# Copies out of PSUM issued on ScalarE ahead of the last pair's remaining activations, and a second buffer for sums of weights, in the seven-product FFN of a hybrid decoder block

## The chip, the cores and the metric

The kernel runs on one core of a Trainium2 chip, as one program without loops at run time. Its engines are TensorE (PE, with weight loads listed as PEld), VectorE (DVE), ScalarE (ACT), GpSimd (POOL) and SyncE (SP, which here issues DMAs only). The metric is the device time of one execution in microseconds; less is better. Engines run their own instructions strictly in the order written, and wait for each other by semaphores.

## The reference

A decoder block for 1024 tokens of width 1024: two token mixers, their merge, and then the part that matters here, a gated FFN with a causal convolution of width 3 along the tokens (`D_FF` = 2816, that is 22 tiles of 128 features for the gate half and 22 for the value half):

```
def conv_ffn(h, w_up, conv_w, conv_b, w_down):
    u = h @ w_up
    T = u.shape[1]
    up = jnp.pad(u, ((0, 0), (CONV_WIDTH - 1, 0), (0, 0)))
    u = sum(up[:, i:i + T] * conv_w[i] for i in range(CONV_WIDTH)) + conv_b
    gate, val = jnp.split(u, 2, axis=-1)
    return (jax.nn.gelu(gate, approximate=True) * val) @ w_down
```

All is float32. A float32 product is made of three products of rounded parts: each operand is split into a high part (`hi`) and the remainder (`lo`), and `mm3` issues high times high, high times low and low times high for each 128 deep slice.

## The kernel before

Features lie on the partitions and tokens along the free dimension, in two halves of 512 tokens. Tile `j` of the gate half and tile `j` of the value half of `w_up` form a pair. Three pairs (`NSTD`) are computed the plain way by `up_std`. The other 19 pairs run in the loop that the change is in. There the product of a 2 by 2 block of weights (two halves of the depth, gate and value) with a 2 by 2 block of activations (two halves of the depth, two token halves) is made with seven block products in place of eight, out of sums of weights and sums of activations. A block product is four slices of depth, three matmuls each, so 12 matmuls, and a pair has 84. The first four of the 19 pairs (`NEAR`) have two of their seven products made earlier and stored in DRAM (`e_d`); they have 60 matmuls and load the two results.

PE's order in a pair is: `pX` first half (weights `w1`), `pZ` (weights `w2`), `pT` (`w2`), `pY` (`w3`), then `pX` second half, `pZ` again (`w3`) and `pT` again (`w4`). The second use of a bank adds to what the first left there, so the first result must have been read before: `s1` is a copy of `pX` by ACT (L1183), `s5` a copy of `pZ` by ACT (L1188), and `s5 = pT + s5` is a DVE addition (L1190). After it come `s1 = pY + s1` (L1192, DVE), the copy of the second `pX` into `ub` (L1195, ACT), the POOL addition of `s1` and `s5` (L1196) and the DVE additions of `pZ` and `pT` to `s1` (L1198, L1200). These give the four tiles of `u`: two feature tiles, two token halves, in `ub`.

Then each of the four tiles goes through `conv`: one ACT activation (L1063) and two DVE operations (L1064, L1066). `gate` takes the two convolved tiles of a token half: gelu on ACT (L1071), their product on DVE (L1072) and a DMA to `f_d`, issued from ACT's own queue (L1073).

The weights of a pair come in by two DMAs on SP's queue (`st1`, L1148, and `st2`, L1150, two buffers each). DVE makes the sums in four operations (`sa` in L1163 and L1164, then in place L1166 and L1167), ACT makes the high parts and POOL or DVE the low parts (`cut`, L1159 and L1160): POOL for `w1`, for `w2` (out of `sa`) and for both halves of `w3`, DVE for `w4`. `sa` has one buffer, so L1163 of the next pair waits until ACT and POOL have read the one before. The low parts of `w1` and `w2` share three buffers, those of `w3` and `w4` two; the high parts of `w1` and `w3` share three, those of `w2` and `w4` two.

The two buffers of `st2` are free again when DVE has made the low part of `w4`; only then does SP issue the load for the next pair but one.

The order on each engine comes from a scheduler that plays the program through its own timing and takes, among what is ready, what has the highest priority. Priority is the place in the program's text, except that the weights' block stands in `tc.high_priority(offset=WPRIO)`, 500 instructions ahead. What runs on the chip is the order so fixed.

Of the kernel before, what the change touches and what calls it, by code (L numbers as in the profile page):

```python
# [9 lines left out]
F32 = mybir.dt.float32  # L10
# [148 lines left out]
def body(tc, nc, xT, xN, pos, wch, wbrw, wbret, wout, wup, wdn, w2a2, gw2, rows, vecs, consts0, consts1, out):  # L159
    V, S, G, PE = nc.vector, nc.scalar, nc.gpsimd, nc.tensor  # L160
    ctx = ExitStack()

    @contextmanager
    def tile_pool(**kw):
        with tc.tile_pool(**kw) as pool:
            yield Lines(pool)

    with ctx:
# [18 lines left out]
        def VC(name):  # L187
            o, n = VOFF[name]
            return vct[:, o:o + n]
# [5 lines left out]
        def bank(name, tag="A"):  # L195
            return psB.tile([128, 512], F32, tag=tag, name=name, bufs=BANKS[tag])
# [69 lines left out]
        wx = pz.tile([128, 2, KT, 128], F32R, tag="BKp", name="w_x")  # L266
# [60 lines left out]
        with pctx, tile_pool(name="p1", bufs=1, reuse_waits="tile", side="right") as p1:  # L327
# [159 lines left out]
            n = gp.tile([128, 512], F32, tag="rt", name="nrot", bufs=1)  # L487
# [551 lines left out]


        bp = ctx.enter_context(tile_pool(name="bp", bufs=1, reuse_waits="tile"))
        ectx = ExitStack()
        b12 = ectx.enter_context(tile_pool(name="b12", bufs=1, reuse_waits="tile"))
        es = ectx.enter_context(tile_pool(name="es", bufs=2, reuse_waits="tile"))

        w3s = ectx.enter_context(tile_pool(name="w3s", bufs=1, reuse_waits="tile"))
        wpools[:] = [(wp, (2, 3, 2)), (w3s, (1, 1, 1)), (wp, (2, 3, 2))]
        f_d = dp.tile([2, FT, 128, 512], F32, name="f_d")
        carry = cp.tile([128, 2 * NSTD, 2], F32, name="carry", bufs=1)
# [5 lines left out]
        def mmb(ps, w, ks, B, first, last):  # L1055
            mm3(ps, [(w[0][:, k, :], w[1][:, k, :], B[n][0], B[n][1]) for n, k in enumerate(ks)],
                first=first, last=last, skip=not first)

        def conv(pool, ub, b, j, src):

            i = j + FT * b
            u = pool.tile([128, 512], F32, tag=f"u{b}", name="u_f")
            S.activation(u, src, AF.Identity, bias=VC("cb")[:, i:i + 1], scale=VC("cw2")[:, i:i + 1])  # L1063
            V.scalar_tensor_tensor(out=u, in0=ub[:, 1:513], scalar=VC("cw1")[:, i:i + 1], in1=u,  # L1064
                                   op0=ALU.mult, op1=ALU.add)
            V.scalar_tensor_tensor(out=u, in0=ub[:, 0:512], scalar=VC("cw0")[:, i:i + 1], in1=u,  # L1066
                                   op0=ALU.mult, op1=ALU.add)
            return u

        def gate(j, hf, u0, u1):  # L1070
            S.activation(u0, u0, AF.Gelu_apprx_tanh)  # L1071
            V.tensor_tensor(out=u0, in0=u0, in1=u1, op=ALU.mult)  # L1072
            nc.scalar.dma_start(f_d[hf, j], u0)  # L1073
# [63 lines left out]
        wx = ctx.enter_context(tile_pool(name="wx", bufs=1, reuse_waits="tile", side="right"))  # L1137
# [3 lines left out]
        fp = fctx.enter_context(tile_pool(name="fp", bufs=2, reuse_waits="tile"))  # L1141
        W8 = [128, 8, 128]
        lh, rh_ = slice(0, 4), slice(4, 8)

        for n, j in enumerate(range(NSTD, FT)):
            with tc.high_priority(offset=WPRIO):
                st1 = wp.tile(W8, F32, tag="ws", name="w_st", bufs=2)
                nc.sync.dma_start(st1, wup[j])  # L1148
                st2 = wx.tile(W8, F32, tag="ws", name="w_st", bufs=2)
                nc.sync.dma_start(st2, wup[j + FT])  # L1150
                sa = wx.tile(W8, F32, tag="sa", name="w_sa")
                if n >= NEAR:
                    w1 = wp.tile(W8, F32R, tag="wh", name="w_hi", bufs=3), wx.tile(W8, F32R, tag="wl", name="w_lo", bufs=3)
                w2 = wx.tile(W8, F32R, tag="wh", name="w_hi", bufs=2), wx.tile(W8, F32R, tag="wl", name="w_lo", bufs=3)
                w3 = wp.tile(W8, F32R, tag="wh", name="w_hi", bufs=3), wp.tile(W8, F32R, tag="wl", name="w_lo", bufs=2)
                w4 = wx.tile(W8, F32R, tag="wh", name="w_hi", bufs=2), wp.tile(W8, F32R, tag="wl", name="w_lo", bufs=2)

                def cut(w, ks, src, eng):
                    S.copy(w[0][:, ks, :], src)  # L1159
                    eng.tensor_tensor(out=w[1][:, ks, :], in0=src, in1=w[0][:, ks, :], op=ALU.subtract)  # L1160
                if n >= NEAR:
                    cut(w1, slice(0, 8), st1, G)
                V.tensor_tensor(out=sa[:, lh, :], in0=st2[:, lh, :], in1=st2[:, rh_, :], op=ALU.add)  # L1163
                V.tensor_tensor(out=sa[:, rh_, :], in0=st1[:, lh, :], in1=st2[:, lh, :], op=ALU.subtract)  # L1164
                cut(w2, slice(0, 8), sa, G)
                V.tensor_tensor(out=st2[:, lh, :], in0=sa[:, lh, :], in1=st1[:, lh, :], op=ALU.subtract)  # L1166
                V.tensor_tensor(out=st1[:, rh_, :], in0=st1[:, rh_, :], in1=st2[:, lh, :], op=ALU.subtract)  # L1167
                cut(w3, lh, st2[:, lh, :], G)
                cut(w3, rh_, st1[:, rh_, :], G)
                cut(w4, lh, st2[:, rh_, :], V)  # L1170
            if n >= NEAR:
                pX = psA.tile([128, 512], F32, tag="a", name="ps_x")
            pZ = bank("ps_z", "B")
            pT = bank("ps_t", "CY"[n % 2])
            pY = bank("ps_y", "AI"[n % 2])
            ub = [fp.tile([128, 1026], F32, tag=f"ub{b}", name="ub") for b in range(2)]
            for b in range(2):
                G.memset(ub[b][:, 0:2], 0.0)
            s1 = fp.tile([128, 512], F32, name="s1")
            s5 = fp.tile([128, 512], F32, name="s5")  # L1180
            if n >= NEAR:
                mmb(pX, w1, range(4), hn2[0][0:4], True, True)
                S.copy(s1, pX)  # L1183
            else:
                nc.sync.dma_start(s1, e_d[n, 0])
                nc.sync.dma_start(ub[0][:, 2:514], e_d[n, 1])
            mmb(pZ, w2, range(4), T1, True, True)
            S.copy(s5, pZ)  # L1188
            mmb(pT, w2, range(4, 8), T3, True, True)
            V.tensor_tensor(out=s5, in0=pT, in1=s5, op=ALU.add)  # L1190
            mmb(pY, w3, range(4), T2, True, True)
            V.tensor_tensor(out=s1, in0=pY, in1=s1, op=ALU.add)  # L1192
            if n >= NEAR:
                mmb(pX, w1, range(4, 8), hn2[0][4:8], False, True)
                S.copy(ub[0][:, 2:514], pX)  # L1195
            G.tensor_tensor(out=ub[1][:, 514:1026], in0=s1, in1=s5, op=ALU.add)  # L1196
            mmb(pZ, w3, range(4, 8), hn2[1][4:8], False, True)
            V.tensor_tensor(out=ub[0][:, 514:1026], in0=pZ, in1=s1, op=ALU.add)  # L1198
            mmb(pT, w4, range(4), T4, False, True)
            V.tensor_tensor(out=ub[1][:, 2:514], in0=pT, in1=s1, op=ALU.add)  # L1200
            for hf in range(2):
                cv = [conv(fp, ub[b][:, 512 * hf:512 * hf + 514], b, j, ub[b][:, 512 * hf + 2:512 * hf + 514])
                      for b in range(2)]
                gate(j, hf, *cv)
        fctx.close()


        n2 = ctx.enter_context(tile_pool(name="n2", bufs=2, reuse_waits="tile", side="right"))
# [101 lines left out]
```

## Time and profile before

| | us |
|---|---|
| median of 3 runs | 1898.92 |
| lowest, highest | 1895.99, 1899.91 |
| the profiled execution | 1902.93 |
| its span, first to last instruction | 1901.1 |
| PE busy in the span | 1787.9 (94%) |
| DVE busy | 1176.8 (62%) |
| ACT busy | 649.7 (34%) |
| POOL busy | 686.1 (36%) |

The profiled execution lies 4.0 us over the median of the runs. PE's busy time counts matmuls that overlap each other; whether PE is waiting is seen from the gaps between the starts of matmuls. The loop of 19 pairs runs from about 1253 to 1630 us of the span, and the steady pairs among them follow one another at equal distances.

### The profile page before, as it was taken

Reading aid. Unit: us, or ns where it says so; the run is one execution under the profiler, and the core shown is the slowest. Engines: PE = TensorE matmul, PEld = TensorE weight load, DVE = VectorE, ACT = ScalarE, POOL = GpSimd, SP = SyncE. Lnnn points to the kernel's source line nnn. Section 1 sums busy time; section 2 is a strip of 40 time slices with the busy share of each in tenths; the row PEclk is TensorE's granted clock in tenths of the full one; section 3 lists DMA queues with packets and bytes.
Section 4 is the critical chain, followed back from the end, with each engine's and each line's share of the span. In section 5 each row is a group of like instructions: output and inputs, shape, how many; then the busy total and the mean of one; then the engine's idle time right before and its main releaser. Section 6 shows DMA issues by size and latency. Waiting matters only on the chain.

```text
span 1901.1 us, 27394 instructions
## 1 busy us (share of the span) xinstructions
PE 1787.9 (94%) x10610; PEld 1450.2 (76%) x10610; DVE 1176.8 (62%) x2067; ACT 649.7 (34%) x993; POOL 686.1 (36%) x492
## 2 busy tenths in 40 slices
PE   8779999999999999999999999888999999999996
PEld 7657778788777778878788777666777777777885
DVE  4786584755666635663445828689888888752413
ACT  6543212111111112332443434544444444443320
POOL 1344523312212221111564744535454454222523
PEclk9989999999999999999999999899999999999998
DMA  8333532433333225455643735332222222664521
GB/s 285 87 113 100 191 83 67 134 90 94 109 100 105 69 89 176 151 177 172 217 154 123 242 106 197 122 135 89 89 67 78 83 73 78 221 210 142 188 92 44
DMA packets 202690, 244.44 MB, mean 129 GB/s; under 512 B 60992, under 2 KB 136256, under 8 KB 201536
## 3 DMA queue, kind: packets, MB, share of 16 engines
q1 hardware_dynamic: 125712, 171.11, 29.4%
q10 hardware_dynamic: 76848, 71.59, 11.5%
q8 instruction: 83, 1.36, 0.3%
q14 instruction: 47, 0.39, 0.1%
HBM read 177.10 MB, written 65.54 MB: 128 GB/s over the span
## 4 chain that ended last, share of the span: by engine, by line
PE 51%; DVE 17%; DMA 9%; issue 5%; ACT 4%; POOL 4%; ACTq 0%; SPq 0%; DVEq 0%; POOLq 0%
PE ps_side L224 7%; PE ps_side L223 7%; PE ps_side L225 7%; DVE u_f L1064 4%; PE ps_dn L225 3%; PE ps_dn L223 3%; PE ps_dn L224 3%; POOL w_lo L1160 2%; DMA w_st<-in_wup_dram 2%; DVE w_sa L1164 2%; DVE w_sa L1163 2%; PE ps_o L224 1%; PE ps_o L225 1%; PE ps_o L223 1%; DVE u_f L1066 1%
## 5 line engine op out<-in xcount | busy, mean ns | idle before, releaser
L217 POOL TENSOR_TENSOR w_lo<-w_st,w_hi 128x1024 fp32r<-128x1024 f32 (+2 forms) x112 | 272.4, 2433 | 513.6 <-ACT w_hi L212 183.8
L212 ACT CAST w_hi<-w_st 128x1024 fp32r<-128x1024 f32 (+2 forms) x162 | 161.7, 999 | 403.6 <-PE ps_side L224 125.8
L224 PE MATMUL ps_side<-hnl,w_hi 128*128 128x512 f32 x640 | 256.3, 400 | 0.0
L223 PE MATMUL ps_side<-hnh,w_hi 128*128 128x512 f32 x640 | 255.6, 399 | 0.0
L225 PE MATMUL ps_side<-hnh,w_lo 128*128 128x512 f32 x640 | 254.8, 398 | 0.0
L223 PEld LDWEIGHTS ps_side<-hnh,w_hi 128*128 128x128 f32 x640 | 121.1, 189 | 26.8 <-issue 1.5
L225 PEld LDWEIGHTS ps_side<-hnh,w_lo 128*128 128x128 f32 x640 | 121.1, 189 | 26.2 <-issue 0.8
L224 PEld LDWEIGHTS ps_side<-hnl,w_hi 128*128 128x128 f32 x640 | 121.0, 189 | 26.3 <-issue 1.5
L217 DVE TENSOR_TENSOR w_lo<-w_st,w_hi 128x1024 fp32r<-128x1024 f32 (+1 forms) x50 | 64.0, 1280 | 83.7 <-ACT w_hi L212 41.5
L1064 DVE SCALAR_TENSOR_TENSOR u_f<-ub,vct,u_f 128x512 f32<-128x512 f32 x88 | 105.5, 1204 | 13.9 <-ACT u_f L1063 13.8
L1160 POOL TENSOR_TENSOR w_lo<-w_st,w_hi 128x512 fp32r<-128x512 f32 (+1 forms) x53 | 106.0, 2024 | 0.0
L1063 ACT ACTIVATE u_f<-ub,vct 128x512 f32<-128x512 f32 x76 | 59.9, 812 | 129.2 <-DVE ub L1198 110.8
L223 PE MATMUL ps_rw<-hnh,w_hi 128*128 128x512 f32 (+1 forms) x224 | 87.8, 392 | 13.2 <-ACT hnh L288 7.0
L224 PE MATMUL ps_rw<-hnl,w_hi 128*128 128x512 f32 (+1 forms) x224 | 86.7, 387 | 0.7 <-DVE hnl L289 0.7
L225 PE MATMUL ps_rw<-hnh,w_lo 128*128 128x512 f32 (+1 forms) x208 | 80.0, 385 | 0.0
L225 PE MATMUL ps_b<-y_hi,w_lo 128*128 128x512 f32 x192 | 75.1, 392 | 1.9 <-DVE w_lo L217 1.2
L223 PE MATMUL ps_b<-y_hi,w_hi 128*128 128x512 f32 x192 | 75.2, 392 | 0.7 <-ACT w_hi L212 0.6
L224 PE MATMUL ps_b<-y_lo,w_hi 128*128 128x512 f32 x192 | 74.8, 390 | 0.0
L223 PE MATMUL ps_dn<-f_k,w_hi 128*128 128x512 f32 (+1 forms) x198 | 72.5, 366 | 0.0
L225 PE MATMUL ps_dn<-f_k,w_lo 128*128 128x512 f32 (+1 forms) x198 | 72.4, 367 | 0.0
L224 PE MATMUL ps_dn<-f_k,w_hi 128*128 128x512 f32 (+1 forms) x198 | 72.2, 366 | 0.0
L223 PE MATMUL ps_z<-b_hi,w_hi 128*128 128x512 f32 x152 | 60.4, 397 | 12.2 <-ACT w_hi L1159 8.0
(418 smaller groups left out, 4342.2 us busy)
## 6 DMA issues: line engine op xcount, KB each, us to landing
w_st<-in_wup_dram SPq DMA_DIRECT2D x54, 512.0 KB, 3.6
w_st<-in_wch_dram SPq DMA_DIRECT2D x52, 512.0 KB, 4.0
w_st<-in_wdn_dram SPq DMA_DIRECT2D x38, 512.0 KB, 4.0
pj_d<-ot ACTq DMA_DIRECT2D x64, 256.0 KB, 2.2
zvg<-pj_d SPq DMA_DIRECT2D x8, 1536.0 KB, 9.2
f_d<-u_f ACTq DMA_DIRECT2D x44, 256.0 KB, 2.1
L<-L_d SPq DMA_DIRECT2D x8, 1344.0 KB, 6.0
w_st<-in_wbret_dram SPq DMA_DIRECT2D x16, 512.0 KB, 3.7
```

Source lines behind the costliest of these rows:

```text
L212: S.copy(hi, st)
L217: eng.tensor_tensor(out=lo, in0=st, in1=hi, op=ALU.subtract)
L223: PE.matmul(ps, wh, xh, start=first and a == 0, stop=False, skip_group_check=skip)
L224: PE.matmul(ps, wh, xl, start=False, stop=False, skip_group_check=skip)
L225: PE.matmul(ps, wl, xh, start=False, stop=last and a == n - 1, skip_group_check=skip)
L1063: S.activation(u, src, AF.Identity, bias=VC("cb")[:, i:i + 1], scale=VC("cw2")[:, i:i + 1])
L1064: V.scalar_tensor_tensor(out=u, in0=ub[:, 1:513], scalar=VC("cw1")[:, i:i + 1], in1=u, op0=ALU.mult, op1=ALU.add)
L1066: V.scalar_tensor_tensor(out=u, in0=ub[:, 0:512], scalar=VC("cw0")[:, i:i + 1], in1=u, op0=ALU.mult, op1=ALU.add)
L1160: eng.tensor_tensor(out=w[1][:, ks, :], in0=src, in1=w[0][:, ks, :], op=ALU.subtract)
L1163: V.tensor_tensor(out=sa[:, lh, :], in0=st2[:, lh, :], in1=st2[:, rh_, :], op=ALU.add)
L1164: V.tensor_tensor(out=sa[:, rh_, :], in0=st1[:, lh, :], in1=st2[:, lh, :], op=ALU.subtract)
```

## The change

Three things are done. The first convolution of a pair, `part(0, 0)`, is traced at the end of its pair as before. The rest of the pair's convolutions and gates become a function `rest`, which is called in the next pair, just behind the copy of `pZ` into `s5` (L1188), within `tc.issue_after(...)`. That adds, for each instruction of `rest` that runs on ACT (activations, gelus and the issues of the two DMAs to `f_d`), an edge which keeps it behind that copy in ACT's order. DVE's instructions of `rest` get no such edge, but their place in the text moves too. After the loop `rest` is called once more for the last pair. Last, `sa` gets a second buffer: for even pairs it lies in the tag `wh` of the pool `w3s`, which held a third set of weights in the plain pairs, and which is now opened below `b12` and `es` and closed after the loop.

```diff
+        w3ctx = ExitStack()
+        w3s = w3ctx.enter_context(tile_pool(name="w3s", bufs=1, reuse_waits="tile"))
         ectx = ExitStack()
         b12 = ectx.enter_context(tile_pool(name="b12", bufs=1, reuse_waits="tile"))
         es = ectx.enter_context(tile_pool(name="es", bufs=2, reuse_waits="tile"))
-        w3s = ectx.enter_context(tile_pool(name="w3s", bufs=1, reuse_waits="tile"))
...
+        def rest():
+            pass
...
-                sa = wx.tile(W8, F32, tag="sa", name="w_sa")
+                sa = (wx.tile(W8, F32, tag="sa", name="w_sa") if n % 2 else
+                      w3s.tile(W8, F32, tag="wh", name="w_sa"))
...
             mmb(pZ, w2, range(4), T1, True, True)
-            S.copy(s5, pZ)
+
+            with tc.issue_after(S.copy(s5, pZ).ins):
+                rest()
             mmb(pT, w2, range(4, 8), T3, True, True)
...
-            for hf in range(2):
-                cv = [conv(fp, ub[b][:, 512 * hf:512 * hf + 514], b, j, ub[b][:, 512 * hf + 2:512 * hf + 514])
-                      for b in range(2)]
-                gate(j, hf, *cv)
+
+            def part(b, hf, j=j, ub=ub):
+                return conv(fp, ub[b][:, 512 * hf:512 * hf + 514], b, j, ub[b][:, 512 * hf + 2:512 * hf + 514])
+
+            def rest(j=j, part=part, u0=part(0, 0)):
+                gate(j, 0, u0, part(1, 0))
+                gate(j, 1, part(0, 1), part(1, 1))
+        rest()
         fctx.close()
+        w3ctx.close()
```

## Rows read from the trace of the kernel before

**Rows 1.** The windows view: length, busy us (count) of PE, PEld, DVE, ACT, POOL, clock.

```profile
1463.77:1484.26 20.49, 19.32 (x85) 15.69 (x84) 17.47 (x20) 9.17 (x14) 10.05 (x9) 1.00 0.21 78
...
1300.00:1320.00 20.00, 15.98 (x63) 12.69 (x62) 18.64 (x22) 9.01 (x13) 12.02 (x8) 0.91 0.28 92
```

**Rows 2.** The waits of PE, 1230 to 1660 us: total, times, longest.

```profile
PE ps_x L223 <- ACT s L1183: 16.8, 14, 2.1
PE ps_z L223 <- ACT w_hi L1159: 8.0, 1, 8.0
...
PE ps_x L223 <- ACT w_hi L1159: 2.9, 1, 2.9
```

**Rows 3.** The timeline of PE, one pair: start, duration, instruction, idle time before.

```profile
1463.77 0.39 PE L223 MATMUL ps_x<-b_hi,w_hi 128*128 128x512 f32 x1
...
1475.98 0.50 PE L223 MATMUL ps_x<-b_hi,w_hi 128*128 128x512 f32 x1 [1.17 <-ACT s L1183]
...
1481.56 0.39 PE L223 MATMUL ps_t<-b_hi,w_hi 128*128 128x512 f32 x1
...
1484.28 0.39 PE L223 MATMUL ps_x<-b_hi,w_hi 128*128 128x512 f32 x1
```

**Rows 4.** The timeline of ACT, the same pair.

```profile
1471.18 0.81 ACT L1063 ACTIVATE u_f<-ub,vct 128x512 f32<-128x512 f32 x1 [7.82 <-DVE ub L1198]
...
1474.85 0.61 ACT L1071 ACTIVATE u_f<-u_f 128x512 f32<-128x512 f32 x1
1475.36 0.56 ACT L1183 COPY s<-ps_x 128x512 f32<-128x512 f32 x1
1475.83 0.58 ACT L1188 COPY s<-ps_z 128x512 f32<-128x512 f32 x1
1478.53 0.93 ACTq L1073 DMA_DIRECT2D f_d<-u_f  x2
1479.49 1.05 ACT L1159 CAST w_hi<-w_sa 128x1024 fp32r<-128x1024 f32 x1 [3.09 <-DVE u_f L1072]
```

**Rows 5.** The timeline of DVE, the same pair.

```profile
1462.57 1.77 DVE L1163 TENSOR_TENSOR w_sa<-w_st 128x512 f32<-128x512 f32 x1 [2.78 <-POOL w_lo L1160]
...
1470.46 0.68 DVE L1198 TENSOR_TENSOR ub<-ps_z,s 128x512 f32<-128x512 f32 x1
...
1472.70 0.68 DVE L1200 TENSOR_TENSOR ub<-ps_t,s 128x512 f32<-128x512 f32 x1
1473.30 0.74 DVE L1066 SCALAR_TENSOR_TENSOR u_f<-ub,vct,u_f 128x512 f32<-128x512 f32 x1
1473.96 0.68 DVE L1160 TENSOR_TENSOR w_lo<-w_st,w_hi 128x512 fp32r<-128x512 f32 x1
...
1479.02 0.68 DVE L1190 TENSOR_TENSOR s<-ps_t,s 128x512 f32<-128x512 f32 x1
```

**Rows 6.** The timeline of POOL, the same pair.

```profile
1460.13 2.41 POOL L1160 TENSOR_TENSOR w_lo<-w_sa,w_hi 128x1024 fp32r<-128x1024 f32 x1 [2.52 <-ACT w_hi L1159]
1462.50 1.29 POOL L1196 TENSOR_TENSOR ub<-s,s 128x512 f32<-128x512 f32 x1
1463.75 6.24 POOL L1160 TENSOR_TENSOR w_lo<-w_st,w_hi 128x512 fp32r<-128x512 f32 x3
```

**Rows 7.** The timelines of POOL and DVE about 1300 us.

```profile
1299.61 2.85 POOL L1160 TENSOR_TENSOR w_lo<-w_st,w_hi 128x1024 fp32r<-128x1024 f32 x1
...
1297.77 2.43 DVE L1072 TENSOR_TENSOR u_f<-u_f 128x512 f32<-128x512 f32 x1
1300.12 0.68 DVE L1192 TENSOR_TENSOR s<-ps_y,s 128x512 f32<-128x512 f32 x1
```

**Rows 8.** DMA issues of the page: count, KB each, us to landing.

```profile
w_st<-in_wup_dram SPq DMA_DIRECT2D x54, 512.0 KB, 3.6
```

**Rows 9.** The timeline of PE about 1314 us.

```profile
1314.19 0.51 PE L223 MATMUL ps_z<-b_hi,w_hi 128*128 128x512 f32 x1 [4.02 <-ACT s L1188]
...
1318.18 0.40 PE L224 MATMUL ps_z<-b_lo,w_hi 128*128 128x512 f32 x1
```

## The prediction

> **What bounds the kernel now.** Take the windows first [rows 1]. A steady pair lasts 20.5 us; PE is busy for 19.32 of them and DVE for 17.47, which leaves neither much room. PE's waits come next [rows 2]: between 1230 and 1660 us nearly all belong to one cause, the second use of `pX`, which waits for ACT's copy of the first into `s1` (L1183), 14 times for 16.8 us. Of the single waits, one of 8.0 us stands at the start of the loop and one of 2.9 us in the early pairs.
>
> The timeline of PE gives the price of a wait [rows 3]. The second `pT` starts at 1481.56 and the next pair at 1484.28: 2.72 us for a product, so 7 x 2.72 = 19.04 us for a pair without waits. From pair to pair it is 1484.28 - 1463.77 = 20.51. The one wait therefore costs 1.47 us a pair; the 1.17 us in its row leave out the refilling of the pipeline.
>
> The timeline of ACT shows who is late [rows 4]. The first `pX` was complete at about 1466.7, but its copy starts at 1475.36, and that of `pZ` at 1475.83. They stand behind activations and gelus of the last pair, and those stood still for 7.82 us until DVE had added `pZ` (L1198). ACT was idle while the copies it needed were ready. After them come two issues to `f_d` (0.93 us), which wait for the products on DVE, and only then the high part of `w2`, with 3.09 us of idle ACT.
>
> The timelines of DVE and POOL show what keeps them [rows 5, 6]. L1163 waits 2.78 us for POOL, which reads the only `sa` until then. L1163 itself takes 1.77 us beside a working POOL, where a like addition takes 0.68.
>
> **The change part by part.** No instruction is added or taken away on any engine; order and one buffer change. I count time from the first `pX` matmul of a pair, without PE's wait: first `pX` ends at 2.72, `pZ` 5.44, `pT` 8.16, `pY` 10.88, second `pX` 13.60, `pZ` 16.32, `pT` 19.04.
>
> *The copies.* With `rest` behind them they start when PE is done: `s1` is complete by about 3.5 and `s5` by 6.2 (0.56 and 0.58 us each [rows 4]). The second `pX` wants `s1` at 10.88, so 7.4 us cover it, and the wait of 1.47 us goes. The ceiling is 14 x 1.47 = 20.6 us.
>
> *What is moved.* Two gelus, three activations and two DMA issues of ACT now start at 6.2, not when L1198 is done. A gelu and an activation take some 1.3 us, so DVE can begin `rest` at 7.6: six L1064 or L1066 at 0.66 and two L1072 at 0.60 (spacings of starts [rows 5]), 5.2 us. Queued behind on DVE are L1190 and L1192, 0.6 each. Who waits is PE: the second `pT` at 16.32 needs L1190. Undisturbed, L1190 is done at 13.4, a margin of 2.9 us. Behind the two issues on ACT stand the next high parts and L1195; nothing of that is needed by PE before the next pair, and the next `s1` copy comes at 19.04 + 2.7, 5 us or more after them. On POOL the small writes L1178 wait for `rest` to release `ub` and stand ahead of low parts; these have the same margin as L1192.
>
> *The second `sa`.* It removes DVE's wait of 2.78 us. What is it worth? In 2.41 of them POOL reads and writes SBUF [rows 6], and a DVE operation with two SBUF inputs started then would have waited for POOL anyway. The rows say so: L1072, started at 1297.77, takes 2.43 us and ends only after POOL's next operation has begun at 1299.61; L1192, with one input in PSUM, takes 0.68 us in the middle of that operation [rows 7]. So the gain from the buffer alone lies between nothing and 2.78 us a pair, and I take nearly nothing: it lets sums go elsewhere in DVE's order.
>
> By the Trainium skill, page "SBUF — State Buffer", section "SBUF: two separate sides", a DVE operation with two SBUF inputs and a GpSimd operation that reads SBUF hold a common port pair in turn, each for its whole length. The trace agrees for the 1.77 and 2.43 us; by this rule the freed wait is worth 0.3 us, by the row of the wait 2.78.
>
> *What then sets the pair's length.* DVE has 11 additions at 0.60 and 8 operations at 0.66, together 11.9 us. POOL alone has two low parts of 1024 columns at 2.37 and three operations of 512 at 1.25 (spacings [rows 6]), 8.5 us. If they only alternate, that is 20.4 us, which is very near the 20.51 seen. What shortens it are the four DVE additions that read PSUM. L1198 and L1200 become ready at 16.32 and 19.04, and POOL is busy from about 16 on with L1196, `w3` and `w1`, so these two can pass: 20.4 - 1.2 = 19.2. Against it works a longer loop: L1192, POOL's L1196 and two halves of `w3` with DVE's three locked operations between (5.4 us), `w4`'s low part, the load of `st2` (3.6 us [rows 8]), the three sums (1.8), `rest` (5.2) with one low part of `w2` in between (2.4), L1190 and L1192 (1.2): 19.7 with handoffs, if the sums stand right ahead of `rest` in DVE's order. Floor 19.04, ends 19.04 and 20.4; I take the middle of the two estimates, 19.45. That saves 1.06 us a pair, 14 x 1.06 = 14.8 us.
>
> *The early pairs.* Two waits stem from the same order: 2.9 us for a high part that ACT makes behind the activations [rows 2], and 4.02 us for the copy L1188 [rows 9]. After the latter ten matmuls take 3.99 us (1314.19 to 1318.18) in place of 2.27, and the granted clock of that stretch is 0.91 [rows 1]: 1.7 us more. Together 8.6 us. But DVE is busy 18.64 of 20 us there, so the additions that PE needs next may be late instead. Bounds 0 and 8.6; I take half, 4.3 us.
>
> *The start.* The 8.0 us ahead of the first `pZ` [rows 2] hang on the first sums, which neither edit makes earlier: 0, with ends of 8.0 us won and, should the new place of the first `sa` wait for a plain product (24 matmuls), 5.4 lost.
>
> *Sum.* 14.8 + 4.3 = 19.1. The profiled execution took 1902.93 us (its span is 1901.1), so 1883.8; it lies 4.0 over the median of the runs, which makes 1879.8.
>
> **The rivals.** A, the forecast: pairs of 19.2 to 20, 1874 to 1889 us, chance 0.44.
>
> B, PE becomes the bound: order falls so well that all 14 x 1.47 and the 8.6 us go, 29.2 us, 1870. For it: 2.9 us of margin at L1190 and 7.4 at `s1`. Against: DVE has hardly an idle microsecond in a pair. Chance 0.26.
>
> C, the port is the bound: DVE and POOL keep alternating without a pass, the pair stays at 20.4, and PE's wait only moves to another place, most likely the second `pT` on L1190. 14 x 0.1 + half of 4.3 = 3.5 us, 1895. For it speaks that the sum is within 0.1 us of the measured pair; against it, L1192 passing a POOL operation. Chance 0.12. The skill's page "Perfetto Trace Analysis", "Identifying the Most-Contended Engine", would have the engine with the highest occupancy improved first; with weight loads for 15.69 us and DVE at 17.47 of 20.5 [rows 1] that is DVE, whose work this change leaves alone, and by that rule C would come true.
>
> D, slower: a new loop through PE. The second `pT`, first `pX` and `pZ` (8.16), the `s5` copy with its handoff (0.8), gelu and activation (1.3), `rest` on DVE (5.2), L1190 (0.7): 16.1 us. Whatever else DVE does or waits for between that copy and L1190 adds to it, and beyond 4.4 us the pair is longer than now. `w2`'s low part on POOL (2.4) and five weight operations (3.0) are 5.4: 21.5 a pair, 14 us lost, 2 won early, 1911. Against it, some of these operations are ready before the copy. Chance 0.12.
>
> E, nothing happens: the copies still stand behind something late on ACT, such as a high part that waits for its buffer. 1899, chance 0.06.
>
> **How the numbers follow.** About 0.2%, 3.8 us, is what can be told from no change. A and B are faster, 0.70, and with a part of C 0.76; the rest of C, E and a little of D are the same, 0.13; D is slower, 0.11. The range runs from 1868, B with a little of the start won, to 1897, which takes in C; E and D, 0.18, stay out. A's own range is 1874 to 1889.
>
> **What would show it.** Right: no wait of `ps_x` for L1183; both copies within 1 us of their products; DVE without the wait of L1163 for POOL; first matmuls of pairs 19.0 to 19.7 us apart; L1198 or L1200 taking 0.68 us while POOL works. C shows as PE waiting for L1190 with pairs of 20.4 us, D as the same wait with longer pairs. I am wrong above all if the fixed order puts sums on DVE between the `s5` copy and L1190.

## The result and the profile after

The changed kernel takes 1921.86 us (median of 4 runs, 1920.30 to 1926.70) where the kernel before, in 4 runs, took 1899.41: a ratio of 1.0117, 95% interval 1.0094 to 1.0140. It is slower by 1.2%. The forecast was 1880 us; the result lies above its range, and the time moved the other way.

Line numbers have moved: `s1` copy L1188, `s5` copy L1194, `pT` addition L1197 (L1190 before), `pY` addition L1199 (L1192), `pZ` and `pT` additions to `ub` L1205 and L1207, sums L1168, L1169, L1171, L1172, high and low parts L1164 and L1165, convolution L1064, L1065, L1067, gelu L1072, gate product L1073, issue to `f_d` L1074.

The windows of two successive steady pairs after, cut at L1199 (columns as in [rows 1]), and the stretch of the early pairs:

```profile
1450.28:1472.37 22.09, 19.34 (x85) 15.69 (x84) 17.75 (x20) 9.18 (x14) 9.99 (x7) 0.99 0.23 72
1472.37:1494.46 22.09, 20.97 (x86) 16.82 (x86) 17.62 (x20) 9.18 (x14) 9.98 (x7) 0.93 0.22 71
...
1300.00:1320.00 20.00, 15.47 (x57) 12.21 (x56) 20.00 (x23) 8.95 (x13) 9.83 (x9) 0.83 0.26 93
```

A steady pair lasts 22.09 us, not 20.49, and DVE is busy in it for nearly what it was before. Where the time went is read from one instruction per pair, the `pY` addition. It starts at these times (L1192 before, L1199 after): pair 0 at 1266.10 and 1264.53, pair 4 at 1336.38 and 1339.85, pair 16 at 1582.07 and 1604.92, pair 18 at 1624.39 and 1641.80. So the start won 1.6 us, the early pairs lost 5.0, twelve steady pairs lost 19.4 (1.61 each), and the last two, which have few or no weights to prepare for a later pair, won 5.4: +17.4, as the spans say (1918.5 against 1901.1). This account goes by DVE. On PE the `pY` product of pair 0 ends 3.4 us earlier than before (1261.65 against 1265.09), and that of pair 4 too (1327.91 against 1331.35): the 5.0 us of the early pairs are how much further DVE has fallen behind PE there.

The waits of PE, 1230 to 1680 us:

```profile
PE ps_t L223 <- DVE s L1197: 29.2, 14, 4.5
PE ps_z L223 <- ACT w_hi L1164: 5.7, 1, 5.7
PE ps_z L223 <- ACT s L1194: 4.5, 1, 4.5
PE ps_z L225 <- POOL w_lo L1165: 3.3, 1, 3.3
```

Against [rows 2], the wait of `ps_x` for the copy into `s1` is gone, 16.8 us. In its place the second `pT` waits for the addition L1197, 29.2 us. The timeline of ACT says that the copies do what they should:

```profile
1478.05 0.58 ACT L1188 COPY s<-ps_x 128x512 f32<-128x512 f32 x1
1480.72 0.59 ACT L1194 COPY s<-ps_z 128x512 f32<-128x512 f32 x1 [2.10 <-PE ps_z L225]
```

The copy of `pZ` waits for PE and for nothing else; in [rows 4] both stood behind activations. Who is late is DVE. Its waits, 1340 to 1600 us:

```profile
DVE w_sa L1168 <- DMA w_st<-in_wup_dram: 35.6, 12, 3.1
DVE u_f L1065 <- ACT u_f L1064: 15.7, 12, 1.3
```

The wait for POOL in [rows 5], 2.78 us a pair, is gone; DVE now waits 3.0 us for the load of `st2` and 1.3 us for an activation, in every pair. The timeline of DVE shows where these two stand in its order:

```profile
1472.37 0.69 DVE L1199 TENSOR_TENSOR s<-ps_y,s 128x512 f32<-128x512 f32 x1
1472.97 0.75 DVE L1067 SCALAR_TENSOR_TENSOR u_f<-ub,vct,u_f 128x512 f32<-128x512 f32 x1
1473.82 1.58 DVE L1073 TENSOR_TENSOR u_f<-u_f 128x512 f32<-128x512 f32 x1
1476.71 1.66 DVE L1065 SCALAR_TENSOR_TENSOR u_f<-ub,vct,u_f 128x512 f32<-128x512 f32 x1 [1.31 <-ACT u_f L1064]
1478.29 0.68 DVE L1205 TENSOR_TENSOR ub<-ps_z,s 128x512 f32<-128x512 f32 x1
1478.89 2.28 DVE L1067 SCALAR_TENSOR_TENSOR u_f<-ub,vct,u_f 128x512 f32<-128x512 f32 x1
1481.10 0.68 DVE L1207 TENSOR_TENSOR ub<-ps_t,s 128x512 f32<-128x512 f32 x1
1481.70 0.67 DVE L1165 TENSOR_TENSOR w_lo<-w_st,w_hi 128x512 fp32r<-128x512 f32 x1
1482.30 0.68 DVE L1172 TENSOR_TENSOR w_st<-w_st 128x512 f32<-128x512 f32 x1
1485.97 2.61 DVE L1168 TENSOR_TENSOR w_sa<-w_st 128x512 f32<-128x512 f32 x1 [2.99 <-DMA w_st<-in_wup_dram]
1488.50 0.68 DVE L1169 TENSOR_TENSOR w_sa<-w_st 128x512 f32<-128x512 f32 x1
1489.22 0.69 DVE L1171 TENSOR_TENSOR w_st<-w_sa,w_st 128x512 f32<-128x512 f32 x1
...
1491.94 0.68 DVE L1197 TENSOR_TENSOR s<-ps_t,s 128x512 f32<-128x512 f32 x1
...
1494.46 0.68 DVE L1199 TENSOR_TENSOR s<-ps_y,s 128x512 f32<-128x512 f32 x1
```

DVE makes the low part of `w4` at 1481.70. That frees the buffer of `st2`; SP issues the next load at 1482.40. With one instruction (L1172) in between, DVE's order has L1168, the first sum of that very load, and behind the sums three operations of `rest` and then the addition that PE needs. The chain of waits closes on itself without PE (start, us, what):

```profile
1473.82 1.60 DVE u_f L1073
...
1475.44 0.33 ACTq L1074
...
1475.87 0.82 ACT u_f L1064
...
1476.71 1.66 DVE u_f L1065
1478.37 0.60 DVE ub L1205
1478.97 2.20 DVE u_f L1067
1481.18 0.60 DVE ub L1207
1481.78 0.61 DVE w_lo L1165
...
1482.40 3.54 DMA w_st<-in_wup_dram
...
1485.97 2.61 DVE w_sa L1168
...
1492.02 0.60 DVE s L1197
...
1495.91 1.61 DVE u_f L1073
```

From L1073 to L1073 is 22.09 us. The links that are not DVE's work are the load with 3.54 us and the way over ACT: the issue to `f_d` must wait for L1073, the activation L1064 stands behind the issue on ACT, and L1065 waits for the activation. L1168 takes 2.61 us in place of 0.68 because POOL's low part of `w2` begins just before it, as the timeline of POOL shows:

```profile
1474.86 5.77 POOL L1165 TENSOR_TENSOR w_lo<-w_st,w_hi 128x512 fp32r<-128x512 f32 x3
1485.64 2.40 POOL L1165 TENSOR_TENSOR w_lo<-w_sa,w_hi 128x1024 fp32r<-128x1024 f32 x1 [5.01 <-ACT w_hi L1164]
```

### The profile page after: what moved, and what is told of

It reads as the page before. It is cut to its first block, busy times and chain, and to the rows that moved or that the text cites. A ratio compares the mean times of both kernels' runs of the same rounds, so it can differ in the third digit from the quotient of the medians.

```text
span 1918.5 us, 27340 instructions
## 1 busy us (share of the span) xinstructions
PE 1796.5 (94%) x10610; PEld 1457.2 (76%) x10610; DVE 1182.0 (62%) x2067; ACT 650.1 (34%) x993; POOL 691.1 (36%) x492
## 4 chain that ended last, share of the span: by engine, by line
PE 49%; DVE 21%; DMA 10%; issue 5%; POOL 3%; ACT 2%; ACTq 0%; SPq 0%; DVEq 0%; POOLq 0%
PE ps_side L224 6%; PE ps_side L223 6%; PE ps_side L225 6%; DVE u_f L1065 3%; DVE u_f L1067 3%; PE ps_dn L225 3%; PE ps_dn L223 3%; PE ps_dn L224 3%; DMA w_st<-in_wup_dram 3%; DVE u_f L1073 2%; DVE w_sa L1168 2%; PE ps_o L224 1%; PE ps_o L225 1%; PE ps_o L223 1%; DVE xprod L627 1%
## 5 line engine op out<-in xcount | busy, mean ns | idle before, releaser
L1065 DVE SCALAR_TENSOR_TENSOR u_f<-ub,vct,u_f 128x512 f32<-128x512 f32 x88 | 85.8, 976 | 29.5 <-ACT u_f L1064 29.5
L1165 POOL TENSOR_TENSOR w_lo<-w_st,w_hi 128x512 fp32r<-128x512 f32 (+1 forms) x53 | 99.5, 1901 | 1.2 <-issue 1.2
L1067 DVE SCALAR_TENSOR_TENSOR u_f<-ub,vct,u_f 128x512 f32<-128x512 f32 x88 | 95.9, 1091 | 0.6
L223 PE MATMUL ps_t<-b_hi,w_hi 128*128 128x512 f32 x152 | 64.9, 427 | 29.2 <-DVE s L1197 29.2
L1165 POOL TENSOR_TENSOR w_lo<-w_sa,w_hi 128x1024 fp32r<-128x1024 f32 x19 | 50.8, 2675 | 107.2 <-ACT w_hi L1164 100.5
L1072 ACT ACTIVATE u_f<-u_f 128x512 f32<-128x512 f32 x44 | 27.5, 626 | 142.5 <-DVE u_f L1067 142.5
L1064 ACT ACTIVATE u_f<-ub,vct 128x512 f32<-128x512 f32 x76 | 59.7, 810 | 41.9 <-DVE u_f L1073 19.3
```

The source lines that it names most:

```text
L223: PE.matmul(ps, wh, xh, start=first and a == 0, stop=False, skip_group_check=skip)
```

## The experiments

The theory: the loss is this closed loop of DVE, and it exists because the two parts of the change together put the sums of weights between the low part of `w4` and `rest`, where their load has just been issued. Rivals: `rest` behind the `s5` copy is by itself too late for PE (D of the prediction); the second `sa` does harm by where it lies in memory; ACT's issues are the main cost. The kernel before took 1898.93 us beside the first four, 1900.85 beside the next four and 1901.94 beside the last. Pair lengths are distances of the `pY` additions; where DVE is not the last to finish they vary from pair to pair, and the distance of the first `pZ` matmuls on PE is given instead.

**e1: the memory order alone.** The kernel before, with only the pool `w3s` moved as in the change; one `sa`, `rest` not moved.

```diff
+        w3ctx = ExitStack()
+        w3s = w3ctx.enter_context(tile_pool(name="w3s", bufs=1, reuse_waits="tile"))
         ectx = ExitStack()
...
-        w3s = ectx.enter_context(tile_pool(name="w3s", bufs=1, reuse_waits="tile"))
...
+        w3ctx.close()
```

> The kernel before, with the pool w3s opened below b12 and es and closed after the loop, and nothing else. Theory: what the changed kernel won ahead of the loop (its first pZ stands at 1245.3 us instead of 1253.6) comes from this move of memory alone, and the loop itself stays as it was: 20.5 us a pair, about 1893 us in all against 1899. Rival: the start moved because the first sums no longer stand behind others, that is by the second sa; then this kernel is within 2 us of the kernel before.

1896.01 us, ratio 0.9980 [0.9964, 0.9995]. Pairs stay at 20.5 us and PE's wait is that of before:

```profile
PE ps_x L223 <- ACT s L1184: 15.4, 13, 2.1
PE ps_z L223 <- ACT w_hi L1160: 6.3, 1, 6.3
```

The first `pZ` starts at 1247.90, against 1253.55 before and 1245.27 in the changed kernel: two thirds of the earlier start come from the place of the pool. In all it is 2.9 us under the kernel before, between the two expectations. Memory does no harm.

**e2: `rest` moved, one `sa`.** The changed kernel without its second buffer.

```diff
-                sa = (wx.tile(W8, F32, tag="sa", name="w_sa") if n % 2 else
-                      w3s.tile(W8, F32, tag="wh", name="w_sa"))
+                sa = wx.tile(W8, F32, tag="sa", name="w_sa")
```

> The changed kernel with one buffer for sa, as before; rest stays behind the copy of pZ. Theory (DVE's loop through the load of st2): the loss is not in the move of rest but in the sums, which the second buffer lets stand right ahead of rest on DVE, where they wait 3.0 us for a load issued just before. With one sa they fall back behind L1199 and find their weights loaded; no wait of DVE for a DMA, pairs of 19.5 to 20.5 us, 1880 to 1895 us in all. Rival (rest starts too late on DVE, whatever stands ahead of it): pairs stay near 22 us, PE still waits 2 us or more on the addition of pT, 1915 us or more.

1881.16 us, ratio 0.9910 [0.9886, 0.9935]; pairs of 19.49 us up to 1486 us, with DVE busy for 19.45 of them, and from 1509 on, behind one longer pair, 19.04 on PE. With one `sa` the sums can't go before POOL has read the last one; in the fixed order they stand behind the `pY` addition (here L1198), and DVE never waits for a load:

```profile
1467.08 0.68 DVE L1198 TENSOR_TENSOR s<-ps_y,s 128x512 f32<-128x512 f32 x1
...
1468.34 1.78 DVE L1167 TENSOR_TENSOR w_sa<-w_st 128x512 f32<-128x512 f32 x1
...
1478.59 0.67 DVE L1164 TENSOR_TENSOR w_lo<-w_st,w_hi 128x512 fp32r<-128x512 f32 x1
```

So `rest` behind the `s5` copy is not too late by itself: that rival falls. The moved half of the change gives what the whole was forecast to give.

**e3: the second `sa` alone.** The kernel before with the pool moved and the second buffer; activations in their old place.

```diff
-                sa = wx.tile(W8, F32, tag="sa", name="w_sa")
+                sa = (wx.tile(W8, F32, tag="sa", name="w_sa") if n % 2 else
+                      w3s.tile(W8, F32, tag="wh", name="w_sa"))
```

> The kernel before with the second sa (and its pool) alone; rest stays at the end of its own pair. Theory: DVE does not wait for the load here, since five operations stand between the low part of w4 and the sums; the copies are still late by the old order, pairs of 20.0 to 20.7 us, 1888 to 1900 us. Rival (the second buffer harms by itself, since sums run beside POOL's low part): pairs of 21 us or more, 1905 us or more.

1879.51 us, ratio 0.9907 [0.9881, 0.9933]: faster than expected. The first `pZ` of the steady pairs start 19.04 us apart on PE, which waits for nothing between 1345 and 1580 us. So the expectation that the copies stay late was wrong: the activations stand in their old order, and with DVE earlier they and the copies behind them are in time. DVE's timeline has slack now:

```profile
1471.89 0.75 DVE L1065 SCALAR_TENSOR_TENSOR u_f<-ub,vct,u_f 128x512 f32<-128x512 f32 x1 [3.87 <-ACT u_f L1064]
...
1483.06 0.69 DVE L1165 TENSOR_TENSOR w_sa<-w_st 128x512 f32<-128x512 f32 x1 [0.31 <-DMA w_st<-in_wup_dram]
1483.67 0.69 DVE L1166 TENSOR_TENSOR w_sa<-w_st 128x512 f32<-128x512 f32 x1
```

The sums stand 4 us behind the low part of `w4` and meet their load just as it lands; they take 0.69 us each where they took 1.77 beside POOL [rows 5]. DVE is busy for 15.16 us a pair (windows view), before for 17.47.

**e4: the whole change, the sums held.** One more edge in the order: the first two sums of pair n stay behind the `pT` addition of pair n-2 on DVE. No other line of the program differs. In the order that follows from it the `pZ` addition also stands ahead of L1065, which waits for an activation, and no longer behind it; e5 leaves these two as they were.

```diff
...
+                with (tc.issue_after(adds[n - 2].ins) if n > 1 else ExitStack()):
+                    V.tensor_tensor(out=sa[:, lh, :], in0=st2[:, lh, :], in1=st2[:, rh_, :], op=ALU.add)
+                    V.tensor_tensor(out=sa[:, rh_, :], in0=st1[:, lh, :], in1=st2[:, lh, :], op=ALU.subtract)
...
-            V.tensor_tensor(out=s5, in0=pT, in1=s5, op=ALU.add)
+            adds.append(V.tensor_tensor(out=s5, in0=pT, in1=s5, op=ALU.add))
```

> The changed kernel, with the first two sums of pair n kept behind the addition of pT (L1197) of pair n-2 in DVE's order. Nothing else differs, and no transfer is sooner. Theory: the load has then 3 us of other DVE work to hide behind and rest starts when ACT feeds it; DVE's wait for the load goes, PE's wait on L1197 goes or falls under 0.5 us, pairs of 19.1 to 19.9 us, 1872 to 1888 us. Rival (rest too late by its own): 22 us a pair, 1918 us. Second rival (the common port of DVE and POOL): the wait for the load goes but the pair stays at 20.4 us, 1893 us.

1877.45 us, ratio 0.9890 [0.9869, 0.9912]; steady pairs of 19.04 us on PE. DVE's waits from 1340 to 1600 us:

```profile
DVE u_f L1065 <- ACT u_f L1064: 4.0, 7, 1.3
...
DVE w_sa L1170 <- DMA w_st<-in_wup_dram: 0.8, 2, 0.5
```

35.6 and 15.7 us have become 0.8 and 4.0, the second `pT` waits 0.2 us in all, and the chain is PE's matmuls at 0.23 us. This edge makes 44 us of difference to the changed kernel: with e5, where the order is kept and only the load is earlier, it shows that the place of the sums, right behind the issue of their load, is the cause.

**e5: a third buffer for `st2`.** The sums keep the place that they have in the changed kernel (held behind the low part of `w4` of pair n-2), but their load can be issued earlier.

```diff
-                st2 = wx.tile(W8, F32, tag="ws", name="w_st", bufs=2)
+                st2 = (wx.tile(W8, F32, tag="ws", name="w_st", bufs=2) if n % 3 else
+                       w3s.tile(W8, F32, tag="ws", name="w_st"))
...
+                with (tc.issue_after(w4lo[n - 2].ins) if n > 1 else ExitStack()):
...
+                w4lo.append(cut(w4, lh, st2[:, rh_, :], V))
```

> The changed kernel with a third buffer for st2 (in the free tag ws of w3s), so that its load can be issued a pair earlier; the sums are kept behind the low part of w4 of pair n-2 in DVE's order, so that they stay ahead of rest (the first sum moves by one place only). Theory (a closed loop on DVE through the load): the wait of 3.0 us goes, every other piece stays, pairs of 19.1 to 19.5 us, 1876 to 1888 us. Rival (the sums themselves and POOL's port ahead of rest are what makes L1197 late, not the load): the wait for the load turns into a wait for the port, pairs of 21 us or more, 1905 us or more.

1882.63 us, ratio 0.9918 [0.9885, 0.9951]; pairs of 19.32 us. The wait for the load is gone, the one for the activation stays:

```profile
DVE u_f L1065 <- ACT u_f L1064: 17.7, 15, 1.3
```

So the place of the sums harms through the load and not through the work that they put ahead of the addition. 22.09 - 19.32 = 2.77 us a pair goes with the load's wait; with that link cut, ACT's 1.31 us weigh little: 19.32 is 0.28 over PE's own 19.04.

**e6: the sums held later still,** behind the `pY` addition, about where e2 has them, with both buffers.

```diff
...
-            V.tensor_tensor(out=s1, in0=pY, in1=s1, op=ALU.add)
+            adds.append(V.tensor_tensor(out=s1, in0=pY, in1=s1, op=ALU.add))
```

> The changed kernel with both sa buffers, the sums kept behind the addition of pY (L1199) of pair n-2, which is where they stand with one sa in the second experiment. Theory: the place in DVE's order decides and not the number of buffers, so it comes out as that experiment did, 19.5 us a pair and 1878 to 1885 us. Rival (the second buffer costs or brings something of its own): more than 5 us away from 1881.

1883.63 us, ratio 0.9915 [0.9887, 0.9943]: in all that of e2 within the intervals, but the expected pairs of 19.5 us did not come. They are 19.00 us (19.04 on PE): the first sum, which here starts right behind the `pY` addition and in e2 one operation later, takes 0.67 us and not 1.78. On the other hand the `pY` product of pair 4 ends on PE at 1327.94, in e2 at 1320.67. So the second buffer does bring something and cost something, and in the total the two cancel. What this run shows is that both buffers do no harm where the sums stand well behind their load; it does not show that their number is without effect.

**e7: `rest` earlier,** behind the copy of `pX` instead of that of `pZ`.

```diff
-                S.copy(s1, pX)
+                with tc.issue_after(S.copy(s1, pX).ins):
+                    rest()
...
-            with tc.issue_after(S.copy(s5, pZ).ins):
-                rest()
+            S.copy(s5, pZ)
```

> The changed kernel, with rest behind the copy of pX (s1) and no longer behind that of pZ (s5), so 2.7 us earlier on ACT; two sa. In DVE's order the sums then stand behind the first operation of rest, and eight operations lie between them and L1197. Theory: what counts is what stands between the low part of w4 and the sums; here only two operations do, so DVE still waits 1.5 to 2.5 us for the load, but rest has begun earlier; pairs of 19.0 to 20.5 us, 1876 to 1895 us. Rival (rest too late by its own): the earlier start alone brings the pair under 19.3 us although the wait for the load stays.

1911.45 us, ratio 1.0056 [1.0038, 1.0074]; pairs of 21.6 us. A miss: I had expected a gain. The wait for the load is 2.3 us a pair, as expected, but both of DVE's waits are still there:

```profile
DVE u_f L1065 <- ACT u_f L1064: 35.6, 12, 3.0
DVE w_sa L1168 <- DMA w_st<-in_wup_dram: 27.1, 12, 2.4
```

It is 10 us under the changed kernel and still over the one before: an earlier start of `rest` does not open the loop. The loop takes another form: the wait on ACT has grown, and the chain now also holds a DMA to `f_d` of 2.01 us.

**e8: `f_d` issued by SP.** The changed kernel, with the two issues a pair taken off ACT's queue; DVE's order is unchanged.

```diff
-            nc.scalar.dma_start(f_d[hf, j], u0)
+            (nc.sync if j >= NSTD else nc.scalar).dma_start(f_d[hf, j], u0)
```

> The changed kernel with the loop's DMAs to f_d issued from SP's queue and not from ACT's; DVE's order is that of the changed kernel. Theory (closed loop): the activation L1064 no longer waits on ACT behind an issue that waits for L1073, DVE's second wait of 1.3 us goes, and since the loop closes through it the pair shortens by the same 1.3 us, to 20.8, while the 3.0 us for the load stay; 14 x 1.3 = 18 us, 1900 to 1908 us in all. Rival (the load alone sets the pair): DVE waits longer for the load by what it waits less for ACT, 22 us a pair, 1918 us or more.

1894.04 us, ratio 0.9971 [0.9951, 0.9992]; pairs of 19.85 us. The direction was right, the size was not: 2.24 us a pair where some 1.3 were expected. DVE's timeline:

```profile
1472.87 2.28 DVE L1165 TENSOR_TENSOR w_lo<-w_st,w_hi 128x512 fp32r<-128x512 f32 x1
...
1478.71 1.15 DVE L1168 TENSOR_TENSOR w_sa<-w_st 128x512 f32<-128x512 f32 x1 [2.96 <-DMA w_st<-in_wup_dram]
```

The wait for the load is the same, 2.96 us. From the `pY` addition to the issue of the load it is 9.3 us in place of 10.0: the 1.31 us are gone, the low part of `w4` now waits for POOL, and others wait less. From the load's landing to the end of the sums it is 2.5 us in place of 3.9: L1168, which now starts later within POOL's low part of `w2`, takes 1.15 us in place of 2.61.

**e9: e4 and e8 together.** The same edit of `f_d`, where the loop is open.

```diff
-            nc.scalar.dma_start(f_d[hf, j], u0)
+            (nc.sync if j >= NSTD else nc.scalar).dma_start(f_d[hf, j], u0)
...
+                with (tc.issue_after(adds[n - 2].ins) if n > 1 else ExitStack()):
...
```

> The changed kernel with two edits together: the sums of pair n stay behind the pT addition of pair n-2 in DVE's order (the version that took 1877.45 us), and the two DMAs to f_d are issued by SP and not by ACT. In the changed kernel the second edit alone gave 2.24 us a pair, some 28 us in all. Theory: what ACT's issues cost is a link of DVE's closed loop; with the sums out of that loop PE is the bound (pairs of 18.9 to 19.1 us) and the same edit is worth nothing: 1874 to 1881 us. Rival: ACT's issues delay the gelus and activations for their own sake, and the edit gains in the early pairs too: 10 us or more, under 1868 us. Second rival: on SP's queue the issues to f_d wait for products and keep back the weight loads behind them: over 1885 us, with DVE's sums waiting for loads.

1876.72 us, ratio 0.9878 [0.9856, 0.9901], against 0.9890 [0.9869, 0.9912] of e4: no difference that these intervals can tell, and the steady pairs are again 19.04 us on PE. What gave 2.24 us a pair inside the loop gives nothing outside it.

## Why the prediction was wrong

**The step that failed is "What then sets the pair's length".** It had the right loop and sized it too low, and then it did not let it decide. The loop was written as L1192, POOL's and DVE's operations (5.4 us), `w4`'s low part, the load, the sums, `rest` with one low part of `w2` in between, L1190 and L1192, "if the sums stand right ahead of `rest` in DVE's order". They stand exactly there. In the rows after it has four stretches:

| stretch | terms of the prediction | after |
|---|---|---|
| `pY` addition to the issue of the load | 0.6 + 5.4 + 0.6 = 6.6 | 1472.37 to 1482.40: 10.03 |
| the load | 3.6 | to 1485.97: 3.57 |
| three sums, with `w2`'s low part | 1.8 + 2.4 = 4.2 | to 1489.91: 3.94 |
| `rest` and the `pT` addition | 5.2 + 0.6 = 5.8 | to 1494.46: 4.55 |
| pair | 20.2 (written as 19.7) | 22.09 |

The mis-sized term is the 5.4 us. I had counted only POOL's operations and DVE's passes between them. In DVE's order there also stand a convolution (0.85) and the last gate product (1.60), then a wait over ACT's queue (1.31), then a convolution (1.66), the `pZ` addition (0.60), another convolution (2.20) and the `pT` addition (0.60): together 8.82, to which the `pY` addition (0.60) and the low part (0.61) come. The queue was in my text ("Behind the two issues on ACT stand the next high parts and L1195"), but the list is not complete: the activation of `part(0, 0)` stands there too, and DVE waits for it. And the text then took the middle, 19.45, between this loop and the sum of port times (19.2). Two such estimates are not averaged: the pair cannot be shorter than the longer one. With the loop's own terms added up, 20.2, the saving would have been 0.3 us a pair.

**The copies.** Right: the wait of `ps_x` is gone, and e2 shows that moving `rest` alone takes the pair to 19.49 us, 0.04 from the forecast, at 1881.16 us in all. That the number is so near is in part luck: it was the mean of two estimates, and in e2 neither load nor loop sets the pair, but DVE's work beside POOL, 19.45 us of it. Nor was the move needed for this wait, since in e3 it goes without it. And in [rows 2] it is half of PE's waits (16.8 of 33.8 us), not nearly all; in the steady pairs it is the only one.

**The second `sa`.** Wrong by the most in kind: "nearly nothing". e3 gives it, with the pool's place, 19 us alone, and e1 says that the place gives some 3 of them. With the freed wait, the sums no longer fall beside POOL's low part: two of them at 0.69 us in place of 1.77 are 2.16 of the 2.31 us by which DVE's busy time falls. What the freed wait is worth apart from that no run shows; DVE stands still for 3.9 us a pair in e3, so it sets nothing there. The half sentence "it lets sums go elsewhere in DVE's order" was the whole danger, and I did not follow it to a place. The two halves of the change each gain about 0.9%, and together they lose 1.2%.

**The early pairs.** Forecast 4.3 won. By DVE's `pY` additions 5.0 were lost, by PE's own `pY` nothing was won or lost. The 2.9 us for the high part are gone, but the wait for the `s5` copy stays (4.5 us), and a second `pT` waits 4.5 us for L1197. DVE is busy for all 20.00 us of that stretch, as the caution said.

**The start.** Forecast 0. The first `pZ` starts 8.3 us earlier, but 1.6 are left at the first `pY` addition. Of the 6.7 us between, about 2.1 are a longer wait for a low part (3.3 us against 1.2); the rest of the way to the end of that `pY` product is 2.8 us longer, with a granted clock of 0.64 over the whole of it (0.87 before); and 1.9 are DVE's, where sums of the third pair now stand ahead of the addition:

```profile
1260.45 2.88 DVE L1169 TENSOR_TENSOR w_sa<-w_st 128x512 f32<-128x512 f32 x1
```

The second buffer has a price ahead of the steady pairs as well. With `rest` moved, the `pY` product of pair 4 ends on PE at 1320.67 us with one `sa` (e2) and at 1327.91 to 1329.06 with two (the changed kernel, e4, e6), or 1322.96 with a third `st2` besides (e5); with `rest` in its old place it ends at 1325.76 with one (e1) and at 1330.60 with two (e3). Through which waits it comes was not followed.

**The rivals.** D named the place (the second `pT` waits for L1190) and came near in time (21.5 us a pair, 1911), but its loop went through PE. That is not what happens: the activations and the gelu that follow the `s5` copy are done by 1484.6 us, and DVE takes them up only at 1489.83, so 5 us of slack lie there; e7 shows that an earlier `rest` does not mend it. C's mechanism, POOL and DVE in turn, is seen in single operations (L1168's 2.61 us), but it doesn't set the pair of 22.09 us; in e2, where DVE hardly stands still, it comes near to what C described, at 19.49 us and not 20.4. By the Trainium skill, page "Perfetto Trace Analysis", "Identifying the Most-Contended Engine", the engine with the highest occupancy, TensorE's being judged by its weight loads, is optimized first. That is DVE in the changed kernel too (17.62 of 22.09 us against 16.82 of weight loads), and the trace agrees that DVE was the place. It does not bear out what I drew from the rule, that C would come true because DVE's work is left alone: DVE stood still for 4.3 of the 22.09 us, and an edge in its order, with the same instructions, took 44 us off (e4). B's time, 1870, was not reached, but its condition was, in the steady pairs of e3, e4 and e9: PE without gaps.

**The warning at the end** ("wrong above all if the fixed order puts sums on DVE between the `s5` copy and L1190") describes what happened. It stood at the end as a condition, and had neither a price of its own nor a chance beyond D's 0.12.

What stays open: why the scheduler's own timing prefers this place for the sums was not measured; that its model expects the load sooner is a guess. A kernel with the start of e2 and the steady pairs of e4 was not run.

## What to carry to other kernels

When the order on the engines is fixed ahead, a freed buffer is an edit of the order too: ask which instruction can now go earlier, what it waits for there, and who stands behind it. Follow the loop once round over all engines, queues and loads, with the present rows for every instruction that stands in it, and let the longest loop be the length; here a load issued one instruction ahead of its first reader put 3 us into each turn. Two edits that gain 0.9% each can lose together, so each is run alone, and one edge in the order (e4) may save the pair of them. It saves them from the loss and does not add them up: 1877.45 us is not clearly less than the 1879.51 of the second buffer alone, since PE's 19.04 us bound the steady pairs of both.

## What the runs showed of the hardware

A longer wait of PE was in most cases followed by a slower stretch of it. The timeline of PE after:

```profile
1470.59 0.50 PE L223 MATMUL ps_t<-b_hi,w_hi 128*128 128x512 f32 x1 [2.75 <-DVE s L1197]
...
1472.12 0.63 PE L223 MATMUL ps_t<-b_hi,w_hi 128*128 128x512 f32 x1
1472.55 0.63 PE L224 MATMUL ps_t<-b_lo,w_hi 128*128 128x512 f32 x1
...
1492.68 0.50 PE L223 MATMUL ps_t<-b_hi,w_hi 128*128 128x512 f32 x1 [1.12 <-DVE s L1197]
...
1514.76 0.50 PE L223 MATMUL ps_t<-b_hi,w_hi 128*128 128x512 f32 x1 [2.71 <-DVE s L1197]
```

After 2.75 us idle, the matmuls start 0.23 us apart at first, and from 1472.12 on 0.43 us apart, for eight of them until 1475.5; the granted clock of that stretch is 0.51, so those matmuls run at the lower of the two levels, 1.2 GHz. In the steady pairs PE's waits for L1197 are of two lengths. None of the five of 1.10 to 1.18 us has a slow stretch behind it; of the six of 2.71 to 2.77 us five have one, and that at 1514.76 has none (0.23 us apart, clock 1.00). A slow stretch delays the next pair's `pT`, which then waits 1.1 to 1.2 us; behind 1514.76, where it was missing, the next wait is 2.77 us again. All these pairs last 22.09 us, so the clock costs nothing here; it uses up time in which PE would have waited.

And a swap of places, with no byte more or less to move, made single DVE operations up to 3.8 times as long: the same sum of 128x512 took 0.68, 1.15, 1.77 and 2.61 us in these kernels, by where it fell in POOL's low parts, while additions that read PSUM took 0.68 inside them, as in [rows 7] (L1205 at 1478.29, inside POOL's 5.77 us from 1474.86).
